# A two-layer decoder trunk on one core: last expert in four strips, w_pg split and router loads elsewhere, a turn of h ahead of a unit's low part

## The chip, the core and the metric

One core of a Trainium2 chip runs the whole program: TensorE (PE, with its weight loads PEld), VectorE (DVE), ScalarE (ACT), GpSimd (POOL) and SyncE (SP), whose queue issues the weight loads. The metric is device microseconds (us) of one execution, lower is better.

## The reference, cut to what matters

256 tokens of width 1024 go through two layers. Each layer is a token mixer, a mixture of experts and a gated per-layer embedding, each added to the residual `h`.

```python
for i in range(DEPTH):                      # 2
    h = h + mixer(rmsnorm(h, norm_mix[i]))  # even: conv + attention, odd: gMLP (w_in_odd, w_out_odd)
    h = h + hier_moe(rmsnorm(h, norm_ffn[i]), ...)   # 32 experts, top-2 of one group of 8
    gate = sigmoid(rmsnorm(h, norm_pl[i]) @ w_pg[i])
    h = h + gate * (p[i] @ w_pe[i])
return rmsnorm(h, final_norm)
# one expert: he = silu(x @ w1[e]) * (x @ w3[e]); y += comb[:, e] * (he @ w2[e])
```

## The kernel before

All code is emitted in one fixed order; each engine gets its instructions in the order in which the program writes them. Weights stream through 25 tiles of 1 MB ("units"), loaded on SP's queue in the order of use (`add_unit`, `emit_loads`); a unit is loaded as soon as the planned number of tiles allows it (`pos["hold"]`).

**Splitting.** The dense products are made of fp32r matmuls with x and w each as high and low part (high·high, low·high, high·low, `mm3`). Each unit of `w_pg` and of the odd mixer is therefore split ahead of use: the high part is a rounding copy on ACT (L130 or L132, `hi`), the low part a subtraction on DVE (L139 or L142, `lo`). `ahead(n)` splits units until `n` (by default `AHEAD = 2`) beyond the number already taken are split; `take` hands out the next unit and raises that number by one. A `w_pg` unit is split in four pieces of 512 columns.

**Mixture of experts (`moe`).** The 32 experts go in eight rounds `q` of four. Each round multiplies the gathered tokens with w1 and w3 (`up`, L923), forms the hidden values `he` (L954), turns them (`turn_hidden`, L960, L963) and multiplies with w2 (`down`, L976). The four experts of a round use four column strips of the array, 32 rows of output each. The result, weighted with the gates, is scattered into the accumulators `acc` by a matmul with the selection matrix (`scatter`, L994 and L996). The eight matmuls of a round's scatter are kept in a list `extra` and are emitted after the next round's `up` with w3. After the last round the kernel weights the output into `oF` (L1105, ACT), splits the first `w_pg` unit between the two halves, and adds with `sums` (L1117) and `add_h` (L448) to `h`.

**Per-layer part (`per_layer`, `proj_rows`).** `h` is turned on PE (L376), its high part `xTH` copied on ACT (L388), its low part `xTL` made on DVE (L392). The turn of the first 512 columns is done at the end of `moe`, that of the second 512 (`hook0`) inside the first `proj_rows`. `proj_rows` takes two units, i = 0 and i = 1; for each it does the token halves tt = 0 and tt = 1. `mid` (the function `rest`: the last `sums`, two `add_h`, two squares L347, rstd L369 and L370) stands between tt = 0 and tt = 1 of unit i = 0, and `hook0` inside tt = 1 of unit i = 0; unit i = 1 needs the columns that `hook0` turns. Unit 1 of `w_pg` is split ahead of i = 0, unit 2 ahead of i = 1.

**Odd mixer.** Its input is turned by `turn_next` (DVE scale L386, ACT copy L388, DVE low L392), the second half of it in `hook`, inside its first `proj_rows`. The first unit's low part (`piece[1]`, DVE L142) is emitted before. Its rstd runs on POOL (L370), behind the loads of `w_raw` and of the router's operands (`router_operands`, L330 to L334), which POOL issues. The activation `v` (L691) needs it.

Of the kernel before, what the change touches and what calls it, by code (L numbers as in the profile page):

```python
# [11 lines left out]
AF = mybir.ActivationFunctionType  # L12
# [34 lines left out]
def body(tc, x, p, norm_mix, norm_ffn, norm_pl, final_norm,  # L47
# [347 lines left out]
    def proj_cols(xH, xL, first=False):  # L395
# [16 lines left out]
                             skip_group_check=first)  # L412
        return ps.rearrange("p (c t) -> p c t", t=T)

    def proj_rows(xH, xL, tag="mm", hook=None, mid=None):

        pss = [psum("pr", tag)[:, 0:512] for _ in range(2)]
        for i in range(2):
            ahead()
            wh, wl = take(512, True)  # L420
            for tt in range(2):
                rows_part(pss[tt], xH, xL, wh, wl, i, tt, slice(0, 512),
                          hook if i == 0 and tt == 1 else None)
                if i == 0 and tt == 0 and mid is not None:
                    mid()
        return pss

    def rows_part(ps, xH, xL, wh, wl, i, tt, c, between=None):
# [245 lines left out]
        return nxt, lps, xc  # L674


    def odd_mixer(norm, xH, xL, w_sT, b_bc, make_w_sT, wr, hook):
        rb = None
        pos["hold"] = HOLD[6]
        v = [big("v0", [P, 4, 512]), big("v1", [P, 4, 512])]  # L680
        ssp = small("ssp", [P, 2, 4])
        for b in range(4):
            pss = proj_rows(xH, xL, ("mm", "y")[b % 2], hook=hook if b == 0 else None)
            if b == 0:
                r = norm.rstd()
            if b == 1:
                rb = norm.rows()
            if b == 2:
                make_w_sT()
            for tt in range(2):  # L690
                nc.scalar.activation(v[tt][:, b, :], pss[tt], AF.Gelu_apprx_tanh,  # L691
                                     scale=r[:, tt:tt + 1])
                sq = act("junk", [P, 512], BF16)
                nc.vector.scalar_tensor_tensor(sq, v[tt][:, b, :], 1.0 / 2048, v[tt][:, b, :],
                                               op0=ALU.mult, op1=ALU.mult,
                                               accum_out=ssp[:, tt, b:b + 1])
        ug = big("ug", [P, 2, 2, 2, T])
        yb = big("yb", [P, 2, 2, 2, T], F32R)

        def proj_u(n):  # L700
            ups = proj_cols(xH, xL)
            u, gt = ug[:, n % 2, 0], ug[:, n % 2, 1]
            nc.vector.tensor_tensor(u, ups, bt(rb), op=ALU.mult)
            nc.scalar.activation(u, u, AF.Gelu_apprx_tanh)
            return u, gt

        ss = small("ssv", [P, 2, 2])
        nc.vector.tensor_tensor(ss, ssp[:, :, 0:2], ssp[:, :, 2:4], op=ALU.add)
        rv = small("rv", [P, 2])
        rstd_of(rv, ss[:, :, 0], ss[:, :, 1])  # L710
        wms = big("wms", [P, 2, 8, P])
        for c in range(2):
            nc.vector.tensor_scalar(wms[:, c], w_sT, rv[:, c:c + 1], None, op0=ALU.mult)
        def gate(i, u):

            u, gt = u
            gps = psum("gps", "tp").rearrange("p (j t) -> p j t", t=T)
            for j in range(2):
                dt = 2 * i + j
                for c in range(2):  # L720
                    vs = slice((dt % 4) * P, (dt % 4) * P + P)
                    nc.tensor.matmul(gps[:, j, c * P:(c + 1) * P], v[c][:, dt // 4, vs],  # L722
                                     wms[:, c, i, :], start=True, stop=True)
            for j in range(2):
                dt = 2 * i + j
                bb = b_bc[:, i, :].unsqueeze(1).to_broadcast([P, 2, P])
                nc.vector.scalar_tensor_tensor(
                    gt[:, j, :].rearrange("p (c t) -> p c t", t=P),
                    gps[:, j, :].rearrange("p (c t) -> p c t", t=P),
                    cols[:, gv_c + dt:gv_c + 1 + dt], bb, op0=ALU.mult, op1=ALU.add)  # L730
            nc.vector.tensor_tensor(gt, gt, u, op=ALU.mult)
            yH, yL = yb[:, i % 2, 0], yb[:, i % 2, 1]
            nc.scalar.copy(yH, gt)
            nc.vector.tensor_tensor(yL, gt, f(yH), op=ALU.subtract)
            return [(yH[:, j, :], yL[:, j, :]) for j in range(2)]

        u = proj_u(0)
        ys = gate(0, u)
        u = proj_u(1)
        ops = [psum("ops", "y") for _ in range(2)]  # L740
        pos["hold"] = HOLD[3]
        nxt = Norm()
        for i in range(8):
            ys_next = gate(i + 1, u) if i < 7 else None
            if i == 6:
                pos["hold"] = HOLD[7]
                emit_loads()
            if i < 7:
                out_acc(ops, ys, i == 0, False, more=i == 6)
            else:  # L750
                lps, xc = finish_mixer(1, ops, ys, nxt, wr)
            if i < 6:
                u = proj_u(i + 2)
            if i == 5:
                pos["hold"] = HOLD[5]
                emit_loads()
            ys = ys_next
        return nxt, lps, xc
# [26 lines left out]
    def moe(li, norm, lps, xc, br):  # L785
# [142 lines left out]
        def places(q):  # L928

            c = slice((q % 2) * P, (q % 2 + 1) * P)  # L930
            s = S[q // 2]
            ps = psum("sl", "tp")
            for tt in range(2):
                nc.tensor.matmul(ps[:, 0:EPG + 1], s[:, tt, c], comb[:, tt, q // 2, :],
                                 start=(tt == 0), stop=(tt == 1))
            for tt in range(2):
                nc.tensor.transpose(ps[:, 128 + tt * P:128 + (tt + 1) * P], s[:, tt, c], ident)
            gt = small("gts", [P, 2])
            nc.vector.tensor_copy(gt[:, 1:2], ps[:, EPG:EPG + 1])
            nc.vector.scalar_tensor_tensor(small("gjunk", [P, EPG]), ps[:, 0:EPG], 1.0,  # L940
                                           own[:, q % 2, :], op0=ALU.mult, op1=ALU.mult,
                                           accum_out=gt[:, 0:1])
            st = act("ST", [P, T], F32R)
            nc.scalar.copy(st, ps[:, 128:128 + T])  # L944
            return gt, st

        def silu(ps, gt):
# [15 lines left out]
            nc.scalar.copy(gs, tp[:, 0:256].rearrange("p (j t) -> p j t", t=P))  # L963
            return gs

        def down(gs, after=None):
            pss = []
            first, ts = take_raw(4, D)
            for n in range(2):
# [3 lines left out]
                for j in range(2):  # L973
                    for e in range(4):
                        s = slice(e * CAP, (e + 1) * CAP)
                        nc.tensor.matmul(ps[s, :], gs[:, j, s], ts[e][:, j, c], start=(j == 0),  # L976
                                         stop=(j == 1))
                if after is not None:
                    after(ps, n)
            drop_raw(first, 4)  # L980
            return pss

# [77 lines left out]
        for q in range(NQ):  # L1060
# [9 lines left out]
            if q == PE_AT:  # L1070
                pe = big("pe", [P, 2, D])
                pT = turn_p(ptok)
                wpe = take(D, True)
                for n in range(2):
                    for tt in range(2):
                        extra.append(lambda n=n, tt=tt: embed(pT, wpe, pe, n, tt))
            p3 = up(3, q, take_raw(4, DE), 4)
            he = hidden(sl, p3)
            if q == 0:
# [13 lines left out]
                emit_loads()  # L1093
        pos["hold"] = HOLD[2]

        gs = turn_hidden(he)
        oF = big("oF", [P, D])
        gt, st = pl.pop(NQ - 1)
        st = f(st)
        nxt = Norm()  # L1100
        first = []

        def after(ps, n):
            c = slice(n * 512, (n + 1) * 512)
            nc.scalar.activation(oF[:, c], ps, AF.Copy, scale=gt[:, 0:1])  # L1105

            if n == 0:
                first.extend(split_pieces(pos["split"], apart=True))
                pos["split"] += 1
            for j in (2 * n, 2 * n + 1):  # L1110
                first[j][0]()
                if n == 0:
                    first[j][1]()

        def sums(tt, n):
            ps = acc[tt][:, n * 512:(n + 1) * 512]
            nc.tensor.matmul(ps, st[:, tt * P:(tt + 1) * P], oF[:, n * 512:(n + 1) * 512],  # L1117
                             start=False, stop=True, skip_group_check=True)
            return ps
        down(gs, after)  # L1120
        xH = big("xTH", [P, KD, T], F32R)
        xL = big("xTL", [P, KD, T], F32R)
        pss = [sums(0, 0), sums(1, 0)]
        add_h(pss[0], 0, 0)
        nxt.square(0, 0)
        add_h(pss[1], 1, 0)
        low0 = turn(0, 0, xH, xL)
        pss.append(sums(0, 1))
        low1 = turn(1, 0, xH, xL)
        nxt.square(1, 0)  # L1130
        low0()
        first[2][1]()
        first[3][1]()
        low1()

        def rest():

# [10 lines left out]
    def per_layer(norm, pe, xH, xL, rest, turn_next=None):  # L1148
# [24 lines left out]
        def quarters(pss, n, piece=None):  # L1173
# [9 lines left out]
                    nc.vector.tensor_tensor(hg[:, tt, c], h[:, tt, c], g[:, c], op=ALU.mult)  # L1183
                nxt.square(tt, n)
            if piece is not None:
                piece[1]()

        pss = proj_rows(xH, xL, "mm", hook=hook0, mid=rest)
        r = norm.r
# [77 lines left out]
    def turn_next(tt, n):  # L1267
        if not xT:
# [8 lines left out]
    nc.gpsimd.dma_start(w_raw, w_s_odd[0].rearrange("g t s -> t g s"))  # L1277
    nc.gpsimd.dma_start(b_bc.rearrange("p g t -> p (g t)"),
                        b_s_odd.rearrange("o g t -> o (g t)").to_broadcast([P, 1024]))
    wr, br = router_operands(1)  # L1280

    def make_w_sT():
        causal = act("causal", [P, P])
        nc.vector.tensor_tensor(causal, upper_b, ident, op=ALU.add)
# [7 lines left out]
    def hook():  # L1292
        for t in range(2):
            turn_next(t, 1)

    norm, lps, xc = odd_mixer(norm, xT["h"], xT["l"], w_sT, b_bc, make_w_sT, wr, hook)
    pe, norm, pxH, pxL, rest = moe(1, norm, lps, xc, br)
    per_layer(norm, pe, pxH, pxL, rest)
    ctx.close()

# [24 lines left out]
```

## Time and profile before

| | us |
|---|---|
| three runs | 743.07, 744.91, 745.07 (median 744.91) |
| the profiled execution, its own time | 743.51 |
| its span, first to last instruction | 741.5 |
| PE busy | 665.1 (90%) |
| DVE busy | 289.3 (39%) |
| ACT busy | 233.3 (31%) |
| mean granted TensorE clock | 0.963 |
| SP's weight queue | 255.35 MB, 85.4% of 16 engines' span |

The profiled execution's time is 2.0 us more than its span. Its records are on a clock that starts with the first instruction. Layer 0's experts end near 320, the odd mixer runs from about 340 to 500, layer 1's experts end near 705, and the rest is the last per-layer part and the final norm.

### The profile page before, as it was taken

How to read it: one execution, taken by the hardware profiler on the slowest of the kernel's cores; microseconds unless marked ns; L12 is line 12 of the kernel's file. 1: busy time of each engine (PE TensorE's matmuls, PEld its weight loads, DVE VectorE, ACT ScalarE, POOL GpSimd, SP SyncE). 2: the span in 40 equal slices, each digit the busy share in tenths (PEclk: the TensorE clock that was granted, in tenths of full speed). 3: DMA queues.
4: the chain of work that ended last, by engine and by line, in shares of the span. 5: the costliest groups of instructions: out<-in, count | busy, mean ns of one | idle time of the engine just before them, and what ended most of it. 6: DMA issues, size and time to landing. Idle time of an engine off the chain costs nothing.

```text
span 741.5 us, 12330 instructions
## 1 busy us (share of the span) xinstructions
PE 665.1 (90%) x5268; PEld 491.2 (66%) x5268; DVE 289.3 (39%) x482; ACT 233.3 (31%) x338; POOL 20.2 (3%) x37
## 2 busy tenths in 40 slices
PE   8999998988889778799999999999898987977795
PEld 8989988754465534358789999987574653633365
DVE  6748733221121210157667765634121220200076
ACT  6446524111112010067543443443101022010084
POOL 3100000000000000000100000000000000000000
PEclk9999999999999998899999999999999999989799
DMA  9994598999999999999971645499999999999931
GB/s 339 367 420 180 173 428 375 382 426 426 423 427 426 426 428 423 425 408 401 378 244 54 198 162 209 146 417 426 426 426 425 426 426 425 427 426 425 420 136 57
DMA packets 61163, 259.18 MB, mean 350 GB/s; under 512 B 4308, under 2 KB 22896, under 8 KB 36272
## 3 DMA queue, kind: packets, MB, share of 16 engines
q1 hardware_dynamic: 59888, 255.35, 85.4%
q0 software_dynamic: 1072, 2.47, 0.9%
q8 instruction: 43, 0.70, 0.3%
q10 hardware_dynamic: 144, 0.52, 0.2%
q14 instruction: 16, 0.13, 0.0%
HBM read 257.28 MB, written 1.05 MB: 348 GB/s over the span
## 4 chain that ended last, share of the span: by engine, by line
PE 58%; DMA 30%; DVE 5%; issue 3%; ACT 3%; POOL 1%; POOLq 0%; SPq 0%; ACTq 0%; DVEq 0%
DMA raw<-in_moe_w_dram 27%; PE pc L411 14%; PE ops L260 9%; PE hps L923 8%; PE gat L865 8%; PE pr L260 6%; PE yps L976 3%; DMA raw<-in_w_pe_dram 3%; DVE wl L139 1%; PE gps L722 1%; PE tp L376 1%; PE lps L467 1%; PE acc L994 1%; PE acc L1117 1%; PE acc L996 1%
## 5 line engine op out<-in xcount | busy, mean ns | idle before, releaser
L923 PE MATMUL hps<-raw,xg 128*32 128x256 f32 x2048 | 141.1, 410 | 36.2 <-DMA raw<-in_moe_w_dram 21.4
L923 PEld LDWEIGHTS hps<-raw,xg 128*32 128x32 f32 x2048 | 69.3, 118 | 107.5 <-DMA raw<-in_moe_w_dram 30.9
L142 DVE TENSOR_TENSOR wl<-raw,wh 128x2048 fp32r<-128x2048 f32 (+1 forms) x45 | 95.7, 2147 | 16.6 <-ACT wh L132 15.2
L976 PE MATMUL yps<-raw,gHL 128*32 128x512 f32 x512 | 69.3, 621 | 23.7 <-ACT gHL L963 17.7
L132 ACT CAST wh<-raw 128x2048 fp32r<-128x2048 f32 (+1 forms) x41 | 74.1, 1826 | 12.2 <-DMA raw<-in_w_in_even_dram 5.7
L944 ACT CAST ST<-sl 128x256 fp32r<-128x256 f32 x16 | 6.0, 372 | 223.6 <-DVE gjunk L940 221.7
L865 PE MATMUL gat<-S,h 128*128 128x256 f32 (+1 forms) x256 | 62.8, 404 | 0.0
L865 PEld LDWEIGHTS gat<-S,h 128*128 128x128 f32 x256 | 62.0, 336 | 1.1 <-issue 0.8
L976 PEld LDWEIGHTS yps<-raw,gHL 128*32 128x32 f32 x512 | 17.0, 113 | 64.3 <-issue 29.7
L987 DVE SCALAR_TENSOR_TENSOR o<-yps,gts,o 128x512 fp32r<-128x512 f32 x28 | 20.2, 748 | 88.7 <-ACT o L986 87.7
L868 DVE TENSOR_TENSOR xg<-gat,gffn 128x512 f32<-128x512 f32 x32 | 22.1, 692 | 61.2 <-PE gat L865 57.6
L260 PE MATMUL pr<-wh,xTH 128*128 128x512 f32 (+1 forms) x152 | 40.8, 390 | 1.6 <-ACT xTH L388 1.3
L411 PE MATMUL pc<-xTH,wh 128*128 128x256 f32 x288 | 42.1, 290 | 0.1
L411 PE MATMUL pc<-xTH,wl 128*128 128x256 f32 x288 | 40.5, 284 | 0.0
L411 PE MATMUL pc<-xTL,wh 128*128 128x256 f32 x288 | 40.3, 283 | 0.0
L260 PE MATMUL pr<-wl,xTH 128*128 128x512 f32 (+1 forms) x152 | 39.6, 383 | 0.4 <-DVE wl L142 0.4
L954 DVE TENSOR_TENSOR he<-sl,hps 128x256 f32<-128x256 f32 x16 | 6.7, 422 | 83.0 <-PE hps L923 83.0
L260 PE MATMUL pr<-wh,xTL 128*128 128x512 f32 (+1 forms) x152 | 39.1, 379 | 0.0
L411 PEld LDWEIGHTS pc<-xTH,wh 128*128 128x128 f32 x288 | 38.5, 196 | 0.9 <-ACT xTH L521 0.3
L986 ACT ACTIVATE o<-yps,gts 128x512 fp32r<-128x512 f32 x28 | 18.2, 684 | 63.6 <-PE yps L976 63.6
L411 PEld LDWEIGHTS pc<-xTH,wl 128*128 128x128 f32 x288 | 37.1, 192 | 0.3
L411 PEld LDWEIGHTS pc<-xTL,wh 128*128 128x128 f32 x288 | 37.1, 192 | 0.0
(228 smaller groups left out, 813.6 us busy)
## 6 DMA issues: line engine op xcount, KB each, us to landing
raw<-in_moe_w_dram SPq DMA_DIRECT2D x192, 1024.0 KB, 19.5
raw<-in_w_in_odd_dram SPq DMA_DIRECT2D x16, 1024.0 KB, 13.2
raw<-in_w_in_even_dram SPq DMA_DIRECT2D x11, 1024.0 KB, 11.7
raw<-in_w_pg_dram SPq DMA_DIRECT2D x8, 1024.0 KB, 12.4
raw<-in_w_out_odd_dram SPq DMA_DIRECT2D x8, 1024.0 KB, 6.1
raw<-in_w_out_even_dram SPq DMA_DIRECT2D x4, 1024.0 KB, 10.8
raw<-in_w_pe_dram SPq DMA_DIRECT2D x2, 1024.0 KB, 20.3
raw<-in_w_in_even_dram SPq DMA_DIRECT2D x2, 512.0 KB, 5.8
```

The costliest lines, as they stand in the source:

```text
L132: nc.scalar.copy(wh[:, c], raw[:, c])
L139: nc.vector.scalar_tensor_tensor(wl[:, c], raw[:, c], cols[:, col + j:col + j + 1], f(wh[:, c]), op0=ALU.mult, op1=ALU.subtract)
L142: nc.vector.tensor_tensor(wl[:, c], raw[:, c], f(wh[:, c]), op=ALU.subtract)
L260: nc.tensor.matmul(ps, x, w, start=start and i == 0, stop=stop and i == 3 * n - 1)
L376: nc.tensor.transpose(tp[:, j * P:(j + 1) * P], h[:, tt, k * P:(k + 1) * P], ident)
L411: nc.tensor.matmul(o, w, xx, start=st, stop=True if first else i % (3 * KD) == 3 * KD - 1, skip_group_check=first)
L865: nc.tensor.matmul(ps[:, k], src[:, tt, k0 + k, :], S[g][:, tt, c0:c1], start=(tt == 0 and k * m % 512 == 0), stop=True, skip_group_check= ...
L868: nc.vector.tensor_tensor(xg[g][:, k0:k0 + n, c0:c1], ps, gffn[:, li, k0:k0 + n].unsqueeze(2).to_broadcast([P, n, m]), op=ALU.mult)
L923: nc.tensor.matmul(ps[e * CAP:(e + 1) * CAP, :], x[:, k, c:c + CAP], ts[e][:, k, :], start=(k == 0), stop=(k == KD - 1))
L976: nc.tensor.matmul(ps[s, :], gs[:, j, s], ts[e][:, j, c], start=(j == 0), stop=(j == 1))
L986: nc.scalar.activation(o[:, 0, c], ps, AF.Copy, scale=gt[:, 0:1])
L987: nc.vector.scalar_tensor_tensor(o[:, 1, c], ps, gt[:, 0:1], f(o[:, 0, c]), op0=ALU.mult, op1=ALU.subtract)
```

## The change

1. In the last round (`q == NQ - 1`) the scatter of the round before is emitted ahead of `up` with w3.
2. The last `down` is written out: three experts in three strips over both halves, evacuated unweighted (ACT and DVE); then the fourth expert in four strips of 256 columns, one column quarter of the output for each strip, evacuated by ACT and DVE in 32-row copies. The gate goes into the selection matrix `st` (`places`).
3. The first `w_pg` unit is split after the first `sums`, not between the halves of `down`; the squares of the first columns come after the turns.
4. In the per-layer part's first `proj_rows`, `ahead(1)` stands ahead of i = 0 and a full `ahead()` directly after `mid`.
5. The low part of the odd mixer's second unit goes into `lows` and is emitted at the end of `hook`, after the turns; the second unit's products are reordered (all with the high part of w first).
6. The router's loads of layer 1 are emitted after the odd mixer's `norm.rstd()`.

```diff
     def proj_rows(xH, xL, tag="mm", hook=None, mid=None):
...
-            ahead()
+            ahead(1 if mid is not None and i == 0 else None)
             wh, wl = take(512, True)
+            if hook is not None and lows and i == 1:
+
+                for lo in (0, 1):
+                    for tt in range(2):
+                        s = slice(tt * P, (tt + 1) * P)
+                        for x, w in ((xH, wl),) if lo else ((xH, wh), (xL, wh)):
+                            for k in range(4):
+                                nc.tensor.matmul(pss[tt], x[:, 4 + k, s], w[:, k, :], start=False,
+                                                 stop=lo == 1 and k == 3)
+                lows.clear()
+                continue
             for tt in range(2):
                 rows_part(pss[tt], xH, xL, wh, wl, i, tt, slice(0, 512),
                           hook if i == 0 and tt == 1 else None)
                 if i == 0 and tt == 0 and mid is not None:
                     mid()
+                    ahead()
...
             if b == 0:
                 r = norm.rstd()
+                late["r"] = router_operands(1)
...
-            nc.scalar.copy(st, ps[:, 128:128 + T])
+            if q < NQ - 1:
+                nc.scalar.copy(st, ps[:, 128:128 + T])
+            else:
+
+                nc.scalar.activation(f(st), ps[:, 128:128 + T], AF.Copy, scale=gt[:, 0:1])
...
+            while q == NQ - 1 and extra:
+                pop()
             p3 = up(3, q, take_raw(4, DE), 4)
...
-        def after(ps, n):
+        fourth, ts = take_raw(4, D)
+        three = slice(0, 3 * CAP)
+        for n in range(2):
             c = slice(n * 512, (n + 1) * 512)
-            nc.scalar.activation(oF[:, c], ps, AF.Copy, scale=gt[:, 0:1])
-
-            if n == 0:
-                first.extend(split_pieces(pos["split"], apart=True))
-                pos["split"] += 1
-            for j in (2 * n, 2 * n + 1):
-                first[j][0]()
-                if n == 0:
-                    first[j][1]()
+            ps = psum("yps", "mm")
+            for j in range(2):
+                for e in range(3):
+                    s = slice(e * CAP, (e + 1) * CAP)
+                    nc.tensor.matmul(ps[s, :], gs[:, j, s], ts[e][:, j, c], start=(j == 0),
+                                     stop=(j == 1))
+            (nc.scalar.copy, nc.vector.tensor_copy)[n](oF[three, c], ps[three, :])
+        s = slice(3 * CAP, P)
+        qs = [psum("yq", "tp")[:, 0:256] for _ in range(2)]
+        for j in range(2):
+            for i in range(4):
+                nc.tensor.matmul(qs[i % 2][i * CAP:(i + 1) * CAP, :], gs[:, j, s],
+                                 ts[3][:, j, i * 256:(i + 1) * 256], start=(j == 0),
+                                 stop=(j == 1))
+        for i in range(4):
+            (nc.scalar.copy, nc.vector.tensor_copy)[i % 2](
+                oF[s, i * 256:(i + 1) * 256], qs[i % 2][i * CAP:(i + 1) * CAP, :])
+        drop_raw(fourth, 4)
...
-        down(gs, after)
+
+        first = split_pieces(pos["split"], apart=True)
+        pos["split"] += 1
...
         add_h(pss[0], 0, 0)
-        nxt.square(0, 0)
+        first[0][0]()
+        first[1][0]()
         add_h(pss[1], 1, 0)
+        first[0][1]()
+        first[1][1]()
         low0 = turn(0, 0, xH, xL)
         pss.append(sums(0, 1))
+        low0()
+        first[2][0]()
+        first[3][0]()
         low1 = turn(1, 0, xH, xL)
-        nxt.square(1, 0)
-        low0()
         first[2][1]()
         first[3][1]()
         low1()
+        for tt in range(2):
+            nxt.square(tt, 0)
...
             if piece is not None:
-                piece[1]()
+                lows.append(piece[1])
...
-    wr, br = router_operands(1)
...
     def hook():
         for t in range(2):
             turn_next(t, 1)
+        for low in lows:
+            low()
```

## Rows read from the trace of the kernel before

**Rows 1.** Windows by stage: us; PE, PEld, DVE, ACT, POOL busy; clock; DMA share; GB/s.

```profile
398.00:494.00 96.00, 96.00 (x637) 88.35 (x636) 61.47 (x64) 39.54 (x35) 0.69 (x1) 1.00 0.53 190
510.00:690.00 180.00, 151.97 (x1460) 91.52 (x1459) 32.75 (x88) 23.57 (x49) 1.30 (x2) 0.95 1.01 426
717.00:729.00 12.00, 12.00 (x58) 10.10 (x58) 10.55 (x16) 9.43 (x18) 0.45 (x1) 1.00 0.01 2
```

**Rows 2.** Timeline of layer 1's last round (start, us, engine, line, what).

```profile
688.18 0.75 DVE L987 SCALAR_TENSOR_TENSOR o<-yps,gts,o 128x512 fp32r<-128x512 f32 x1 [2.09 <-ACT o L986]
...
692.25 5.95 PE L923 MATMUL hps<-raw,xg 128*32 128x256 f32 x58 [1.66 <-DMA raw<-in_moe_w_dram]
...
698.12 0.50 PE L994 MATMUL acc<-o,ST 128*128 128x512 f32 x1
...
698.23 0.42 DVE L954 TENSOR_TENSOR he<-sl,hps 128x256 f32<-128x256 f32 x1 [9.30 <-PE hps L923]
...
699.85 0.40 PE L996 MATMUL acc<-o,ST 128*128 128x512 f32 x1
...
700.57 0.37 ACT L963 COPY gHL<-htp 128x256 f32<-128x256 f32 x1 [12.42 <-PE htp L960]
...
702.18 0.16 PEld L976 LDWEIGHTS yps<-raw,gHL 128*32 128x32 f32 x8 [1.04 <-DMA raw<-in_moe_w_dram]
702.64 0.13 PEld L976 LDWEIGHTS yps<-raw,gHL 128*32 128x32 f32 x4 [0.30 <-issue]
...
705.74 0.30 PEld L1117 LDWEIGHTS acc<-oF,ST 128*128 128x128 f32 x2 [0.84 <-ACT wh L130]
```

**Rows 3.** Timeline of layer 0's last round: three experts' strips, no fourth.

```profile
315.78 1.06 PE L976 MATMUL yps<-raw,gHL 128*32 128x512 f32 x6 [0.52 <-ACT gHL L963]
```

**Rows 4.** Timeline from layer 1's `sums` to the second unit of `proj_rows`.

```profile
707.76 0.69 DVE L448 TENSOR_TENSOR h<-h,acc 128x512 f32<-128x512 f32 x1 [0.17 <-PE acc L1117]
...
710.74 2.55 ACT L130 ACTIVATE wh<-raw,cols 128x512 fp32r<-128x512 f32 x4
...
711.49 2.74 DVE L139 SCALAR_TENSOR_TENSOR wl<-raw,cols,wh 128x512 fp32r<-128x512 f32 x4
...
714.14 1.28 DVE L448 TENSOR_TENSOR h<-h,acc 128x512 f32<-128x512 f32 x2
714.92 0.63 ACT L347 ACTIVATE junk<-h 128x512 bf16<-128x512 f32 x1 [1.62 <-DVE h L448]
...
716.30 1.05 ACT L388 CAST xTH<-tp 128x512 fp32r<-128x512 f32 x2
...
716.92 1.19 PE L260 MATMUL pr<-wh,xTH 128*128 128x512 f32 x4
```

**Rows 5.** Windows: the end of layer 0's routing, and the gather after it.

```profile
121.30:123.40 2.10, 0.33 (x5) 0.22 (x4) 1.65 (x8) 0.00 (x0) 0.00 (x0) 1.00 1.00 414
123.80:126.80 3.00, 3.00 (x16) 3.00 (x16) 0.00 (x0) 0.00 (x0) 0.00 (x0) 0.50 1.01 426
```

**Rows 6.** Timeline at the start of the odd mixer.

```profile
354.14 2.28 DVE L142 TENSOR_TENSOR wl<-raw,wh 128x2048 fp32r<-128x2048 f32 x1
...
357.73 1.19 PE L260 MATMUL pr<-wh,xTH 128*128 128x512 f32 x4 [1.26 <-ACT xTH L388]
...
363.37 0.89 POOL L331 DMA_DIRECT2D wr<-in_router_f_dram  x1 [5.42 <-issue]
363.71 0.15 DVE L369 SCALAR_TENSOR_TENSOR msq<-ss 128x2 f32<-128x2 f32 x1
...
365.37 0.72 POOL L370 TENSOR_TENSOR rstd<-msq,mhalf 128x2 f32<-128x2 f32 x1
...
366.12 1.27 ACT L691 ACTIVATE v<-pr,rstd 128x512 f32<-128x512 f32 x2 [3.35 <-POOL rstd L370]
...
369.23 1.20 PE L260 MATMUL pr<-wh,xTH 128*128 128x512 f32 x4 [0.32 <-ACT wh L132]
...
371.56 1.20 PE L260 MATMUL pr<-wl,xTH 128*128 128x512 f32 x4 [0.22 <-DVE wl L142]
```

More of the change, by code (lines that the diff above doesn't have):

```diff
@@ L413, in proj_cols @@
         return ps.rearrange("p (c t) -> p c t", t=T)
+    lows = []
     def proj_rows(xH, xL, tag="mm", hook=None, mid=None):
@@ L674, in even_mixer, with odd_mixer @@
         return nxt, lps, xc
-    def odd_mixer(norm, xH, xL, w_sT, b_bc, make_w_sT, wr, hook):
+    def odd_mixer(norm, xH, xL, w_sT, b_bc, make_w_sT, late, hook):
         rb = None
@@ L750, in odd_mixer @@
             else:
-                lps, xc = finish_mixer(1, ops, ys, nxt, wr)
+                lps, xc = finish_mixer(1, ops, ys, nxt, late["r"][0])
             if i < 6:
@@ L964, in turn_hidden, with down @@
             return gs
-        def down(gs, after=None):
+        def down(gs):
             pss = []
@@ L977, in down @@
                                          stop=(j == 1))
-                if after is not None:
-                    after(ps, n)
             drop_raw(first, 4)
@@ L1097, in moe @@
         oF = big("oF", [P, D])
-        gt, st = pl.pop(NQ - 1)
-        st = f(st)
+        st = f(pl.pop(NQ - 1)[1])
         nxt = Norm()
-        first = []
-        def after(ps, n):
+        fourth, ts = take_raw(4, D)
+        three = slice(0, 3 * CAP)
+        for n in range(2):
             c = slice(n * 512, (n + 1) * 512)
-            nc.scalar.activation(oF[:, c], ps, AF.Copy, scale=gt[:, 0:1])
-            if n == 0:
-                first.extend(split_pieces(pos["split"], apart=True))
-                pos["split"] += 1
-            for j in (2 * n, 2 * n + 1):
-                first[j][0]()
-                if n == 0:
-                    first[j][1]()
+            ps = psum("yps", "mm")
[16 more added lines that the diff above has]
+        drop_raw(fourth, 4)
         def sums(tt, n):
@@ L1294, in hook @@
             turn_next(t, 1)
-    norm, lps, xc = odd_mixer(norm, xT["h"], xT["l"], w_sT, b_bc, make_w_sT, wr, hook)
-    pe, norm, pxH, pxL, rest = moe(1, norm, lps, xc, br)
+        for low in lows:
+            low()
+    norm, lps, xc = odd_mixer(norm, xT["h"], xT["l"], w_sT, b_bc, make_w_sT, late, hook)
+    pe, norm, pxH, pxL, rest = moe(1, norm, lps, xc, late["r"][1])
     per_layer(norm, pe, pxH, pxL, rest)
```

## The prediction

> **What bounds the kernel now.** I read first the table of stages. In the odd mixer PE is busy for all of its 96 us at full clock, while the DMA engines have half their time free; in the experts it is the other way round, the weight stream runs at 426 GB/s with a DMA share of 1.01; in the last per-layer part PE is busy for 12.00 of 12.00 us again [rows 1]. So time moves only in two ways: what PE does or waits for after a layer's last w2 unit has landed, and what PE waits for in the odd mixer. A shift at layer 0's end is carried by the odd mixer to the start of layer 1's experts, whose length the stream sets; a shift after layer 1's last landing goes straight to the end. I then read the timeline of the three places that the change touches, engine by engine, each time asking what ended PE's wait.
>
> The sum is made against the profiled execution, 743.51 us (span 741.5 and 2.0 around it). It lies 1.4 under the median of the runs, 744.91, and within their spread of 2.0; I add nothing for that.
>
> **Parts 1 and 2: the last round.** In layer 1 PE waits until 692.25 for the fourth w3 unit. The second half of `o` is ready at 688.18 + 0.75 = 688.93, so the scatter that is moved ahead of `up` fits into that wait; it costs nothing there (if the unit were not late, it would cost its 2.0 us where it stands). At its old place it took from 698.12 to about 700.1, between `up` and the turn of `he` [rows 2]. Now the turn can start when `he` is done, 698.23 + 0.42 = 698.65, instead of at 699.85, so `down` starts at 699.85 instead of 701.0. Its units land 1 MB at 426 GB/s apart, 2.46 us; the fourth at 702.18, so the third at 699.7 and all three are there. Before, everything after 702.18 waited for the fourth: eight rounds of strips, a round every 0.13 + 0.30 = 0.43 us [rows 2], 3.44 us, until `sums` at 705.74.
>
> Now the three strips need the same eight rounds, 699.85 + 3.44 = 703.3. The fourth expert's four strips of 256 columns have no row of their own; half of 0.43 for half the columns, twice for each of two k halves, gives an estimate of 0.9: 704.2, long after its landing. Then comes a copy that nothing hides, since `sums` needs it: 0.37 on ACT (as gHL) or 0.42 on DVE (as he, both 128x256 [rows 2]), with some 0.15 to start. `sums` can begin at 704.8. Gain 0.95 us in each layer. Bounds: 0.4 if both strips' copies of an engine are awaited, 1.3 if start-up is nothing. Folding the gate into `st` replaces one ACT copy by another of that size, behind the same DVE result: nothing.
>
> The rounds of three strips are the uncertain row. The one stretch with three strips alone shows six matmul records (two rounds) in 1.06 us [rows 3], 0.86 by the rounds above plus a drain, so I take full overlap. The Trainium skill ("TensorE: Matmul & The Clock Gate", section "Measured speedup vs the span model") gives a speedup of only 2.38 for three column strips; by it the three strips would take 4.3 us instead of 3.44, and the sum below would be 0.9 us higher in each layer.
>
> **Parts 3 and 4: splitting w_pg.** Here I count from the start of `sums`, T (705.74 before). Before, unit i = 1 of `proj_rows` began at 716.92, T + 11.2, and PE was hardly idle on the way; unit 1's casts on ACT (710.74) and low parts on DVE (711.49) ran beside PE's first products [rows 4]. In the changed order:
>
> DVE ends the second `add_h` at T + 2.7 (707.76 + 0.69). Behind it now stand four low parts of the first unit and two xTL, which partly stood before `sums`: six at 0.69 (2.74 / 4) = 4.1, until T + 6.85. PE in that time loses about 0.2 for xTL and the last wh piece, so the last `sums` ends near T + 7.5. The two `add_h` of `rest` at 0.64 [rows 4] follow: the first until T + 7.5, the second from T + 7.7 (after `sums`) to 8.35. ACT's second square then runs from about T + 8.5 to 9.2 (two squares took 716.30 - 714.92 = 1.38).
>
> Now comes the point. `ahead()` after `mid` is called when one unit has been taken, and splits to two beyond: units 1 **and** 2. So eight casts of 2.55 / 4 = 0.64 us stand on ACT, 5.1 us, from T + 9.2 to 14.3. Behind them, in ACT's order, stand the two xTH copies of `hook0`, 1.05 for both [rows 4]. Before, only unit 1's casts were ahead of them, and those were done while DVE was still busy; unit 2's came after. The first xTH is done at T + 14.9. PE has finished both token halves and the eight transposes at T + 11.1, and its next product needs that copy. DVE has the eight low parts ahead of xTL as well, one 0.69 after its cast; xTL comes at about T + 16.0, 0.2 after PE wants it. So PE stands still for 3.8 us, and unit i = 1 begins 3.7 later than T + 11.2 and ends 3.9 later. In both layers. Unit 2 is then split early, but PE had no wait for it before (12.00 of 12.00 busy [rows 1]), so nothing comes back.
>
> Bounds for that stall: 3.4 if PE is late by 0.4 itself, 4.6 if ACT starts 0.7 later behind the squares. I take 3.9, nearest to the rows.
>
> A wait also has a price after it. After a stretch with 0.33 of 2.10 us busy, the granted clock was 0.50 for three us of full PE work, 1.2 instead of 2.4 GHz [rows 5]; three us at half speed lose 1.5. In the changed kernel PE does nothing for 3.8 us and then has dense work at once, so I add 1.5 in each layer (bounds 0 and 2.5).
>
> **Part 5: the turn in the odd mixer.** PE waited 1.26 us at 357.73 for xTH, whose DVE scale stood behind a low part of 2.28 [rows 6]. With the turn first, xTH is there at about 356.4, when PE comes. But the two turns take DVE until about 359.2 (each a scale, a wait for the copy, a low part: some 2.05), the unit's low part then until 361.5; PE, reordered, has done its sixteen products with the high part at 360.3 and waits 1.2 for it. The stall changes its place and its size hardly: I take 0 (bounds: 1.3 gained, 0.3 lost). The next unit's low part on DVE follows at the same time as before.
>
> **Part 6: the router's loads.** POOL issues them with long pauses (5.42 us before one) and takes rstd at 365.37 only, though its input is ready at 363.71 + 0.15; ACT stands 3.35 us before `v`, and the casts behind `v` arrive late at PE, which waits at 369.23 and 371.56 [rows 6]. Without the loads, rstd comes about 1.5 us earlier, and both waits go. They are 0.32 and 0.22 us on PE, with slower starts behind them; between 0.5 and 1.4 I take 0.9. The four loads then stand behind rstd on POOL; the next thing there is the rstd of `v`, which needs the whole first half of the odd mixer, and the operands are wanted only at its end, over 100 us later. That covers them; without the cover a pause of 5 to 6 us each would show.
>
> **Sum.** Each layer: -0.95 + 3.9 + 1.5 = +4.45. Twice that, -0.9 for part 6: +8.0. 743.5 + 8.0 = 751.5 us, slower.
>
> **Rivals.**
> (a) *The clock holds after the stalls.* For it: the wait of 1.04 us at 702.18 was followed by rounds at full speed [rows 2]. Against: what stands in [rows 5], and the length of 3.8. 743.5 + 2 x 2.95 - 0.9 = 748.5; with the clock falling after one of two, 750.0.
> (b) *Only one unit is split after `mid`,* if I miscount `ahead`. ACT would be free at T + 11.75, xTH at 12.4, a stall of 1.3 and about 1.5 lost per layer: 743.5 + 2 x 0.55 - 0.9 = 743.7, no change. The count in the code speaks against it.
> (c) *The copies are not held up, and the change does what its parts promise,* because the casts find idle time on ACT before the squares. Then -2 x 0.95 - 0.9 = -2.8: 740.7, faster. It decides when the stall is under 1.4 us per layer, that is when no more than about four of the eight casts stand ahead of the copies. Against it: ACT keeps its written order in the trace, it stood 3.35 us before `v` with casts right behind [rows 6].
> (d) *Three strips do not overlap fully:* 1.06 for two rounds [rows 3] makes 4.24 instead of 3.44, 0.8 more per layer, 753.1. The 1.06 contains a drain, so I give it little. The 2.38 of the Trainium skill (same page and section) points the same way; that the three experts alone took 1.06 rather than 0.86 does not settle it.
>
> **Chances.** The forecast 0.46 (own range 750 to 754); (a) 0.27; (d) and other losses beyond it 0.10; (b) and partial stalls 0.08; (c) 0.09. A change of 0.3%, 2.2 us, is about what this measurement can tell. Faster is (c), 0.09; within it (b), 0.08; slower the rest, 0.83. The range from 746.5 to 755.5 holds the first two, most of (d) and half-size stalls.
>
> **What would show it.** In layer 1: the scatter before 692, `sums` near 704.8, eight casts L130 in a row right after the squares with xTH behind them, PE idle for 3 to 4 us with ACT xTH as what ended it, the same near 331 to 335 in layer 0, and a granted clock of 0.5 after each. At 357 PE's wait shrinks and one of about 1.2 for a low part follows; `v` starts near 364.7. It is wrong if xTH of `hook0` follows the squares directly, or if PE has other work there.

## The result and the profile after

The changed kernel takes 752.12 us in the median of four runs (750.65 to 753.77), against 744.77 in four runs of the kernel before: a ratio of 1.0104 with a 95% interval of [1.0074, 1.0134], so about 1% slower. Its profiled execution took 753.17 us (span 751.4). The forecast was 751.5, in a range from 746.5 to 755.5. Every ratio below is to runs of the kernel before that were made together with those of the kernel in question.

Between the two profiled executions the span grows by 9.9 us. Marks that both traces have, in order, share it out (`rb` is the small product L361 in the odd mixer, the gather the first product of layer 1's experts with the selection matrix):

| stretch, in each kernel from mark to mark | before | after | difference |
|---|---|---|---|
| start to `sums` of layer 0 | 320.88 | 321.24 | +0.4 |
| `sums` to unit i = 1 of `proj_rows`, layer 0 | 11.19 | 14.64 | +3.45 |
| unit i = 1 to `rb` in the odd mixer | 43.25 | 44.17 | +0.9 |
| `rb` to the gather of layer 1 | 129.76 | 130.20 | +0.4 |
| that gather to `sums` of layer 1 | 200.66 | 199.90 | -0.8 |
| `sums` to unit i = 1, layer 1 | 11.18 | 14.65 | +3.5 |
| unit i = 1 to the first store of the output | 18.50 | 20.47 | +2.0 |
| first store to the end | 6.08 | 6.13 | +0.05 |

First the timeline of the changed kernel in layer 1's last round (start, duration, engine, line, what; in brackets the idle time before it and what ended it); it answers to [rows 2].

```profile
692.00 0.50 PE L1013 MATMUL acc<-o,ST 128*128 128x512 f32 x1 [0.21 <-DVE o L1004]
...
696.94 6.51 PE L938 MATMUL hps<-raw,xg 128*32 128x256 f32 x58 [1.80 <-DMA raw<-in_moe_w_dram]
...
703.49 0.42 DVE L973 TENSOR_TENSOR he<-sl,hps 128x256 f32<-128x256 f32 x1 [11.54 <-PE hps L938]
...
704.56 0.37 ACT L982 COPY gHL<-htp 128x256 f32<-128x256 f32 x1 [13.40 <-PE htp L979]
704.99 0.15 PEld L1128 LDWEIGHTS yps<-raw,gHL 128*32 128x32 f32 x6 [0.71 <-ACT gHL L982]
...
705.44 0.12 PEld L1128 LDWEIGHTS yps<-raw,gHL 128*32 128x32 f32 x3 [0.31 <-issue]
...
708.45 1.04 PE L1135 MATMUL yq<-raw,gHL 128*32 128x256 f32 x14
...
709.54 0.75 ACT L1139 COPY oF<-yq 32x256 f32<-32x256 f32 x2 [2.00 <-PE yq L1135]
709.59 0.88 DVE L1139 COPY oF<-yq 32x256 f32<-32x256 f32 x2 [0.22 <-PE yq L1135]
710.15 1.95 PE L1145 MATMUL acc<-oF,ST 128*128 128x512 f32 x4 [0.67 <-DVE oF L1139]
```

The scatter is over before the fourth w3 unit lands at 696.94, the turn and `down` follow `he` at once, a round of three strips takes 0.12 + 0.31 = 0.43 us like one of four, and the last copies (0.75 / 2 on ACT, 0.88 / 2 on DVE) stand bare before `sums`, which waits for one of each, as forecast. From the fourth unit's landing to `sums` it is 13.21 us, against 13.49 before. In layer 0 it is 321.24 - 308.74 = 12.50, against 320.88 - 307.51 = 13.37. The difference between the layers is `up`: 6.51 us here, at a granted clock of 0.55, and 3.64 in layer 0, at 1.00:

```profile
308.74 3.64 PE L938 MATMUL hps<-raw,xg 128*32 128x256 f32 x58 [1.82 <-DMA raw<-in_moe_w_dram]
```

Now the timeline of the changed kernel from layer 1's squares to the second unit, the answer to [rows 4].

```profile
718.65 0.63 ACT L347 ACTIVATE junk<-h 128x512 bf16<-128x512 f32 x1 [0.56 <-DVE h L462]
...
719.28 4.99 ACT L130 ACTIVATE wh<-raw,cols 128x512 fp32r<-128x512 f32 x8
...
719.53 1.03 PE L376 MATMUL tp<-ident,h 128*128 128x128 f32 x8
...
720.02 5.39 DVE L139 SCALAR_TENSOR_TENSOR wl<-raw,cols,wh 128x512 fp32r<-128x512 f32 x8 [0.45 <-ACT wh L130]
...
720.32 1.17 PE L260 MATMUL pr<-wl,xTH 128*128 128x512 f32 x4
724.18 1.05 ACT L388 CAST xTH<-tp 128x512 fp32r<-128x512 f32 x2
...
724.80 1.20 PE L260 MATMUL pr<-wh,xTH 128*128 128x512 f32 x4 [3.31 <-ACT xTH L388]
...
725.33 1.28 DVE L392 TENSOR_TENSOR xTL<-tp,xTH 128x512 fp32r<-128x512 f32 x2
726.07 0.87 PEld L260 LDWEIGHTS pr<-wh,xTL 128*128 128x128 f32 x4 [0.51 <-DVE xTL L392]
```

The second square ends, and eight casts follow in one row of 4.99 us. The xTH copy stands behind them in ACT's order, and PE, which has done the eight transposes and the last products of the first unit by 721.49 (720.32 + 1.17), waits 3.31 us for it. The low part xTL comes late as well: the products with it start 726.07 - 724.80 = 1.27 us after the first product of the unit, against 717.95 - 716.92 = 1.03 before. Layer 0 has the same rows: eight casts from 330.37, xTH at 335.26, and again a wait of 3.31. Windows of the changed kernel over this wait and the products after it, in both layers (us; PE, PEld, DVE, ACT, POOL busy; granted clock; DMA share; GB/s), show what follows.

```profile
331.60:335.80 4.20, 0.97 (x5) 0.45 (x3) 4.20 (x8) 4.20 (x9) 0.00 (x0) 1.00 1.05 404
336.00:339.40 3.40, 3.33 (x10) 2.38 (x11) 1.69 (x3) 1.80 (x3) 0.00 (x0) 0.73 1.05 404
339.40:342.80 3.40, 3.40 (x13) 2.69 (x13) 1.36 (x2) 0.69 (x1) 0.00 (x0) 0.77 1.05 410
720.50:724.70 4.20, 0.99 (x5) 0.47 (x3) 4.20 (x8) 4.20 (x9) 0.00 (x0) 1.00 0.00 0
725.00:728.40 3.40, 3.33 (x11) 2.33 (x11) 2.62 (x5) 3.37 (x6) 0.00 (x0) 0.75 0.02 5
728.40:731.80 3.40, 3.40 (x13) 2.72 (x12) 3.29 (x6) 1.48 (x3) 0.00 (x0) 0.75 0.00 0
```

With the wait over, PE is busy throughout, but part of that time runs at the lower level (1.2 GHz): 3.40 x 0.27 + 3.40 x 0.23 = 1.7 us lost in layer 0, 2 x 3.40 x 0.25 = 1.7 in layer 1.

Last, the timeline of the changed kernel in the odd mixer, the answer to [rows 6].

```profile
362.31 1.20 PE L430 MATMUL pr<-wh,xTH 128*128 128x512 f32 x4
...
367.22 2.11 PE L430 MATMUL pr<-wl,xTH 128*128 128x512 f32 x8 [0.81 <-DVE wl L142]
...
369.59 0.71 POOL L370 TENSOR_TENSOR rstd<-msq,mhalf 128x2 f32<-128x2 f32 x1 [14.54 <-DVE msq L369]
...
380.05 0.38 PE L361 MATMUL rb<-ident,rstd 128*128 128x128 f32 x2
```

The wait of 1.26 us for xTH is gone, one of 0.81 for the low part stands behind it, rstd follows its input at once, and no product waits until `rb`. From the first product of the odd mixer to `rb` it is 380.05 - 355.19 = 24.86 us, against 375.32 - 349.42 = 25.90 before: 1.04 us less.

### The profile page after: what moved, and what is told of

Its sections match the earlier page's. It is cut to its first block, busy times and chain, and to the rows that moved or that the text cites. A ratio compares the mean times of both kernels' runs of the same rounds, so it can differ in the third digit from the quotient of the medians.

```text
span 751.4 us, 12377 instructions
## 1 busy us (share of the span) xinstructions
PE 667.8 (89%) x5284; PEld 493.5 (66%) x5284; DVE 292.4 (39%) x488; ACT 234.1 (31%) x340; POOL 20.2 (3%) x37
## 3 DMA queue, kind: packets, MB, share of 16 engines
HBM read 257.28 MB, written 1.05 MB: 344 GB/s over the span
## 4 chain that ended last, share of the span: by engine, by line
PE 59%; DMA 31%; DVE 5%; ACT 3%; issue 1%; POOLq 0%; POOL 0%; SPq 0%; ACTq 0%; DVEq 0%
DMA raw<-in_moe_w_dram 30%; PE pc L411 13%; PE pr L260 10%; PE ops L260 9%; PE hps L938 8%; PE gat L880 7%; PE yps L995 2%; DVE wl L139 2%; PE acc L1145 1%; PE lps L481 1%; PE gps L737 1%; PE yps L1128 1%; PE tp L376 1%; DVE wl L142 1%; PE acc L1011 1%
## 5 line engine op out<-in xcount | busy, mean ns | idle before, releaser
L995 PE MATMUL yps<-raw,gHL 128*32 128x512 f32 x448 | 56.0, 596 | 22.0 <-ACT gHL L982 17.2
L995 PEld LDWEIGHTS yps<-raw,gHL 128*32 128x32 f32 x448 | 13.7, 109 | 54.3 <-issue 25.2
```

## The experiments

The theory that they test: the eight casts ahead of the copies are the loss, through PE's wait and through the clock after it; the last round gives back some 0.9 us in each layer, part 6 about 1 us once, part 5 nothing. The rivals are that one unit's casts cost as much, that the wait costs nothing beyond itself, and that the loss lies in another part.

**One unit instead of two behind `mid`.**

```diff
                     mid()
-                    ahead()
+                    ahead(1)
```

> The changed kernel, but only w_pg unit 1 is split after mid; unit 2 is split ahead of i = 1, as before. Theory (the eight casts ahead of hook0's xTH copies are the cost): four casts of 0.63 fewer, so the first xTH comes 2.5 us earlier; PE's wait ahead of i = 1 falls from 3.3 to about 0.9 us, the granted clock stays at 1.0 after it, and each layer is 4 us shorter: 744.5 (743.5 to 746). Rival (the fourth expert's strips and the copies in front of sums are the cost): about 752, as the changed kernel.

743.14 us, a ratio of 1.0001 [0.9986, 1.0016] to the kernel before; the median lies 0.4 us below the range expected. Between the medians one argument is worth 752.12 - 743.14 = 9.0 us, but they are of two sets of runs, and the ratios make it 7.7. In the traces it is 58.81 - 54.52 = 4.29 us from `sums` to `rb` in layer 0 and 35.12 - 30.89 = 4.23 from `sums` to the first store in layer 1, together 8.5. The timeline of this kernel in layer 1:

```profile
713.16 2.55 ACT L130 ACTIVATE wh<-raw,cols 128x512 fp32r<-128x512 f32 x4
...
715.62 1.04 ACT L388 CAST xTH<-tp 128x512 fp32r<-128x512 f32 x2
...
716.23 1.20 PE L260 MATMUL pr<-wh,xTH 128*128 128x512 f32 x4 [0.88 <-ACT xTH L388]
```

Four casts leave a wait of 0.88 us, after which the clock stays at 1.00. From the fourth w3 unit to `sums` it is 12.46 and 12.53 us, so the last round gives its 0.91 and 0.96 here. That gain, the remaining wait and part 6 come to about nothing in sum.

**The split at its old place in `proj_rows`** (part 4 undone).

```diff
-            ahead(1 if mid is not None and i == 0 else None)
+            ahead()
...
                     mid()
-                    ahead()
```

> The changed kernel with the old place of the splits in the per-layer part: unit 1 ahead of i = 0, unit 2 ahead of i = 1. Theory: no casts stand between the squares and hook0's xTH copies. But unit 1's low parts then stand on DVE ahead of the two add_h of rest, which come about 2.7 us later, so PE's transposes wait: i = 1 at about T + 12.5 instead of T + 14.65, no fall of the clock. 744.5 (743 to 746.5). Rival (the cost is in the other parts): about 752.

745.81 us, 1.0016 [0.9997, 1.0035], inside what was expected. Without part 4 most of the loss is gone, so it does not come from the first unit's new place (part 3). But the old order does not bring the other gains to the end either: two rows of this kernel's timeline in layer 1 show unit 1's low parts on DVE, with `add_h` behind them, and PE's transposes wait 0.88 us for that.

```profile
713.05 2.74 DVE L139 SCALAR_TENSOR_TENSOR wl<-raw,cols,wh 128x512 fp32r<-128x512 f32 x4 [0.43 <-ACT wh L130]
...
716.53 1.16 PE L376 MATMUL tp<-ident,h 128*128 128x128 f32 x8 [0.88 <-DVE h L461]
```

In its layer 0 a part of the last `down` ran at a lower clock (0.78 from 316.0 to 321.5, against 1.00 in the changed kernel), and `sums` came 14.20 us after the fourth w3 unit; in layer 1 it was 12.55.

**Part 4 alone on the kernel before.**

```diff
-            ahead()
+            ahead(1 if mid is not None and i == 0 else None)
...
                     mid()
+                    ahead()
```

> The kernel before with part 4 alone: ahead(1) ahead of i = 0 and a full ahead() after mid. Theory: eight casts between the squares and hook0's xTH copies; PE waits about 3.4 us ahead of i = 1 in each layer and runs 1.7 us longer after it at a granted clock of 0.5. 5 us per layer: 755 (752 to 757), so more than the whole change costs. Rival (the cost comes from other parts, the casts are hidden): 744 to 746.

754.54 us, 1.0153 [1.0136, 1.0170]: this edit alone costs more than the whole change. The timeline of this kernel in layer 1 shows the row of eight and the wait, the same in layer 0 (at 335.20):

```profile
719.10 5.00 ACT L130 ACTIVATE wh<-raw,cols 128x512 fp32r<-128x512 f32 x8
...
724.62 2.07 PE L260 MATMUL pr<-wh,xTH 128*128 128x512 f32 x4 [3.31 <-ACT xTH L388]
```

Behind the same wait less is lost here than in the changed kernel: from unit i = 1 to `rb` it is 44.56 us against 43.25 before, from unit i = 1 to the first store 19.84 against 18.50, so 1.3 us in each layer for the clock and a late xTL together.

**The wait filled with work that nobody needs.** The changed kernel, with products into an unused tile just where PE waits.

```diff
             wh, wl = take(512, True)
+            if mid is not None and i == 1:
+                fill = psum("fill", "y")
+                for _ in range(56):
+                    nc.tensor.matmul(fill[:, 0:P], ones_b, ones_b, start=True, stop=True)
```

> The changed kernel with 56 added matmuls of ones (128 columns, bf16, into an unused accumulator) just ahead of unit i = 1, where PE waits. They add no result; they keep PE busy for about 3.1 of the 3.3 us. Theory (1.7 us of each layer's loss is the half clock after the wait): the clock stays at 1.0 and i = 1 to the end is 1.7 us shorter in each layer: 748.8 (747.5 to 750). Rival (the whole loss is the wait itself and late xTL): 752, or a little more if the added matmuls run past the wait.

750.18 us, 1.0085 [1.0051, 1.0118], 0.2 us above the range expected. Unit i = 1 begins as late as in the changed kernel (14.69 us after `sums`), so the copies are as late as they were; only the clock differs. The same windows of this kernel, to be set beside those above:

```profile
331.60:335.80 4.20, 4.01 (x61) 3.53 (x59) 4.20 (x8) 4.20 (x8) 0.00 (x0) 1.00 1.05 405
336.00:339.40 3.40, 3.33 (x14) 2.43 (x14) 1.58 (x3) 1.85 (x4) 0.00 (x0) 1.00 1.06 407
...
725.00:728.40 3.40, 3.40 (x16) 2.79 (x16) 3.29 (x5) 2.49 (x5) 0.00 (x0) 1.00 0.02 5
```

From `sums` to `rb` it is 57.22 us instead of 58.81, from `sums` to the first store 33.56 instead of 35.12: 1.6 us in each layer is the price of the clock. In the medians the difference is 1.9 us instead of 3.2, and the intervals overlap; the trace settles it, the times alone would not.

**The other parts, each alone on the kernel before:** part 6, part 5, and part 1 (`while q == NQ - 1 and extra: pop()` ahead of `up`).

> The kernel before with part 6 alone, the router's loads behind the odd mixer's rstd. Theory: rstd runs 0.3 us after its input, v begins 1.5 us earlier, PE's waits for ACT wh and DVE wl in the second block go, and all after it is 1.0 us earlier: 743 (ratio about 0.9986). Rival (POOL's lateness is hidden): no such shift in the trace, ratio 1.000.

Part 6: 742.47 us, 0.9991 [0.9981, 1.0000]. In the trace `sums` to `rb` falls from 54.44 to 53.31, by 1.13 us, since rstd now starts at once:

```profile
363.76 0.71 POOL L370 TENSOR_TENSOR rstd<-msq,mhalf 128x2 f32<-128x2 f32 x1 [13.66 <-DVE msq L369]
```

> The kernel before with part 5 alone, the turn ahead of the unit's low part and the products reordered. Theory: PE's wait of 1.26 us for xTH goes and a wait of about 0.8 to 1.2 us for the unit's low part comes, the second block begins at the same time within 0.2 us: ratio 1.000. Rival (the turn was the bound): 1.2 us less, ratio 0.9984.

Part 5: 742.29 us, 0.9985 [0.9976, 0.9995]. That is a miss, as the theory gave this part nothing. PE's waits change places as foreseen, in its timeline in the odd mixer:

```profile
361.42 2.12 PE L430 MATMUL pr<-wl,xTH 128*128 128x512 f32 x8 [0.81 <-DVE wl L142]
```

But `sums` to `rb` falls by 1.05, to 53.39. The timeline of POOL in the same kernel shows where it may come from:

```profile
346.86 0.95 POOL L1290 DMA_DIRECT2D w_raw<-in_w_s_odd_dram  x1 [14.27 <-PE pr L260]
348.73 0.56 POOL L1291 DMA_DIRECT2D wsb<-in_b_s_odd_dram  x1 [0.92 <-PE pr L260]
354.72 0.89 POOL L330 DMA_DIRECT2D wr<-in_router_c_dram  x1 [5.43 <-issue]
361.03 0.89 POOL L331 DMA_DIRECT2D wr<-in_router_f_dram  x1 [5.42 <-issue]
...
363.78 0.71 POOL L370 TENSOR_TENSOR rstd<-msq,mhalf 128x2 f32<-128x2 f32 x1 [0.77 <-DVE msq L369]
```

The load of `w_raw` goes out at 346.86; before, it stood at 348.83. The loads behind it move too, the router's by 2.34 us, so POOL has issued the last one at 363.0 and is free when rstd's input comes; rstd starts at 363.78, against 365.37. In the trace part 5 thus removes the same lateness of rstd as part 6, by another way.

> The kernel before with part 1 alone, the scatter ahead of the last up. Theory: he comes 1.8 us or more earlier, but down still waits for the fourth w2 unit and has 3.5 us of work behind its landing, so sums stays where it was, within 0.3 us of 13.4 after the fourth w3 unit's landing: ratio 1.000. Rival (the scatter's 2 us stood on the chain): sums 1.5 us earlier per layer, ratio 0.996.

Part 1: 744.62 us, 1.0018 [1.0007, 1.0028]. The scatter is early, but from the fourth w3 unit to `sums` it is still 13.37 and 13.51 us: in the timeline `down` starts sooner, and then waits 1.41 us for its last unit, behind which all rounds still stand.

```profile
699.48 1.20 PE L976 MATMUL yps<-raw,gHL 128*32 128x512 f32 x6 [0.52 <-ACT gHL L963]
702.09 3.62 PE L976 MATMUL yps<-raw,gHL 128*32 128x512 f32 x26 [1.41 <-DMA raw<-in_moe_w_dram]
```

Its runs are 1 us above those before; the one traced execution (span 741.4) does not show where.

**Why part 5 alone gains.** The idea: the load goes out earlier because of the place of its tile. The edit on the kernel before allocates `w_raw` ahead of `wsb`.

```diff
+    w_raw = big("w_raw", [P, 8, P])
     wsb = big("wsb", [P, 2, 8, P])
     w_sT, b_bc = wsb[:, 0], wsb[:, 1]
-    w_raw = big("w_raw", [P, 8, P])
```

> The kernel before with nothing changed but the order in which the two tiles wsb and w_raw are taken. Theory (part 5 alone gained because POOL's first load, of w_raw, could be issued 2 us earlier into a tile that came free earlier, so that the router's loads were through before rstd): w_raw's load goes out near 346.9 instead of 348.8, rstd runs 0.3 us after its input, and the second block and all after it come 1.0 us earlier, though PE's wait of 1.26 us for xTH stays: ratio 0.9986. Rival (part 5 gained on PE): no shift, ratio 1.000.

744.38 us, 1.0004 [0.9995, 1.0013]. The load goes out at 349.13, after the same wait of 16.23 us, and rstd is late as before (365.70). The swap did not set the load free, so it says nothing on what an earlier load brings. What in part 5 frees that tile sooner stays open.

**Parts 5 and 6 together on the kernel before.**

> The kernel before with parts 5 and 6. Theory: both remove the same lateness of rstd, so together they bring what each brings alone, the odd mixer's second product 1.05 us earlier: ratio 0.9986. Rival (each has a gain of its own): 2.1 us, ratio 0.997.

742.99 us, 0.9988 [0.9979, 0.9997]. `sums` to `rb` is 53.38, as with either alone (53.39 and 53.31): the two gains are one.

**A version with the copies ahead of the squares and of unit 2.** The changed kernel, where the casts of unit 1 follow the turns, three of its low parts follow `add_h`, the fourth the turns of `hook0`, the last squares and rstd follow the turns of `hook0`, and unit 2 stands ahead of i = 1.

```diff
                 if i == 0 and tt == 0 and mid is not None:
+                    pcs = split_pieces(pos["split"], apart=True)
+                    pos["split"] += 1
+                    for hi, _ in pcs:
+                        hi()
                     mid()
-                    ahead()
+                    for _, lo in pcs[:3]:
+                        lo()
+                    tail.append(pcs[3][1])
...
                 turn(t, 1, xH, xL)()
+            for lo in tail:
+                lo()
+            tail.clear()
+            for t in range(2):
+                norm.square(t, 1)
+            norm.rstd()
```

> The changed kernel with the per-layer part's first unit pair in another order: unit 1's four casts directly after the turns of moe, the squares of the first columns behind them, three of unit 1's four low parts behind the add_h of rest, then hook0's turns, the last low part, the squares of the second columns and rstd, and unit 2 ahead of i = 1 as before. Theory: no cast and no square stands between add_h and hook0's xTH copies, so i = 1 begins at about T + 11.2, 3.5 us earlier than in the changed kernel and 1 us earlier than with one unit after mid, in each layer; with the last round's and the router's gain 2 to 3 us under the kernel before: 741.5 (740.5 to 743). Rival (PE waits for other things there, low parts above all): as e1, 743 to 744.

742.67 us, 0.9984 [0.9972, 0.9996]. Unit i = 1 begins 11.2 us after `sums` without a wait, as before the change, and the last round keeps its gain. A new wait in the odd mixer takes part of it: 0.51 us for a cast at 350.41, since the load of the sigmoid's table now comes later on ACT. So the next kernel issues that table load ahead of the copies of `hook0`:

> The reordered kernel (e8) with the sigmoid's table load moved ahead of hook0's copies, where ACT stood idle for 1.26 us. Theory: the first sigmoid comes 1.3 us earlier, the casts behind it too, and the wait of 0.51 us on PE at the last w_pg unit's end of layer 0 goes: 0.6 us under e8, ratio to the kernel before about 0.9977. Rival (that wait has another cause): as e8, 0.9984.

741.03 us, 0.9964 [0.9951, 0.9978], the fastest of all, though its interval overlaps that of the reordered version. The wait of 0.51 us is gone, and `sums` to `rb` falls from 54.05 to 53.29. Its timeline in layer 1 shows the load where ACT has time, and the copy right behind it:

```profile
711.82 1.28 ACT L1183 ACT_TABLE_LOAD   x1
...
713.23 1.06 ACT L388 CAST xTH<-tp 128x512 fp32r<-128x512 f32 x2
```

Last, the reordered version without its early scatter (the `while` of part 1 taken out):

> The reordered kernel (e8) with the scatter of the round before back behind up, part 1 undone. Theory: he waits behind the scatter again, down starts 1.9 us later, and with the strips' own work and copies behind it sums comes 13.4 us after the fourth w3 unit, as in the kernel before, instead of 12.5; 0.8 us per layer: ratio about 1.0005. Rival (the strips alone bring the gain): 12.5 us and ratio 0.9984.

744.22 us, 1.0005 [0.9996, 1.0014], against 0.9984 with it. From the fourth w3 unit to `sums` it is 13.29 us in layer 0 and, with `up` at 6.40 us, 705.42 - 691.06 = 14.36 in layer 1. The strips without the early scatter gain nothing, as the early scatter without the strips gained nothing. Part 3 was not run alone.

## Why the prediction was right

**The eight casts (3.9 in each layer): right, and the main cost.** The count of `ahead` decided it. Four casts leave a wait of 0.88 us and no change of the time, eight a wait of 3.31 and some 8 to 9 us; part 4 alone is slower than the whole change. Measured were 3.45 and 3.47, with about 0.25 more where xTL comes late behind eight low parts: 3.7. PE stood still for 3.31 and not 3.8, since it came to the copy at 721.49 - 710.15 = 11.3 us after `sums` and not at 11.1, and the copy itself a quarter of a microsecond sooner. Filled PE time does not help the copies, an earlier copy does.

**The clock after the wait (1.5 in each layer): right.** The row of [rows 5] was enough to foresee it. In the changed kernel two readings give the price: 1.7 from the windows of the granted clock, 1.6 from the kernel whose wait was filled. With part 4 alone it was at most 1.3 behind the same wait; why it differs is open. It is the difference between forecast and rival (a), which falls with it. The wait of 1.04 us that spoke for (a) stands in the row of weight loads; PE itself was busy for 4.67 of the 4.90 us from 700.9.

**The last round (-0.95 in each layer): the mechanism right, the size conditional.** It gave 0.87 in layer 0 and 0.28 in layer 1 of the profiled execution; 0.91 and 0.96 in the kernel with one unit. The working took `up` as it stood. With `up` at 3.64 to 5.2 us the stream decides, and `sums` comes 12.4 to 12.6 us after the fourth unit, save in the layer 0 where `down` ran at the lower clock (14.20); at 6.51 us PE decides, and most of the gain is lost. That the two halves of this step need each other was in the working (the turn starts earlier, the three strips use it) and is shown by the kernels with one of them. The rounds of three strips took 0.43 us, so rival (d) falls. The Trainium skill ("TensorE: Matmul & The Clock Gate", section "Measured speedup vs the span model") gives a speedup of 2.38 for three column strips; an estimate by it is 0.43 x 3 / 2.38 = 0.54 us for a round, and the measured 0.43 decides here.

**Part 5 (0): right in the sum by luck, wrong on its own.** The wait for xTH went, and 0.81 came in place of the 1.2 expected. What the working didn't see is that with this edit POOL's load of `w_raw` goes out 2 us sooner. Alone, the part is worth 1.05 us in the trace. That parts 5 and 6 together bring no more than either shows that it is the gain that part 6 has already; the sum does not change, but no step of the working said so.

**Part 6 (-0.9): right.** 1.04 in the change and 1.13 alone in the trace. Its size is that of the noise in the times, so only the trace shows it.

**The sum.** The terms as measured, -0.87 - 0.28 + 2 x 3.7 + 2 x 1.7 - 1.05, make +8.6 (with 1.05 for parts 5 and 6), against +8.0 forecast; the gain of the last round was 0.75 less than forecast, the clock cost 0.4 more, the casts 0.4 less. The profiled executions differ by 9.7, the medians by 7.35. What the trace shows beside the terms lies in code that the change doesn't touch: +1.13 up to the first gather, +0.4 behind `rb`, and some -0.5 in layer 1's stream; no experiment tells it from the spread between executions. Rival (b) is the first experiment, whose 743.14 lies 0.6 below the 743.7 that it was given. Rival (c) falls with the wait of 3.31 us; it needed the casts to find idle time, and its 740.7 is about what the version with the early table load reaches (741.03) by taking the casts out of the way.

## What to carry to other kernels

When a split or a cast is moved behind other work, count all of its instructions on its engine up to the next copy that PE waits for, and with a "keep two ahead" helper count what it does at its new place, not at the old one. A wait of PE can cost more than its length: here 3.31 us of it were followed by 1.3 to 1.7 us lost to the lower granted clock, 0.88 us by none, and work put into the wait kept the clock up. Two edits that remove the same lateness don't add; measure them together before summing them, and look at the one mark behind both.

## What was not expected of the hardware

The clock of `up` in the last round differed between layers and executions of like code: 58 recorded products took 3.64 us in some, at a granted clock of 1.00, and 4.96 to 6.51 in others, at 0.55 to 0.73. The early scatter fills a part of PE's waits ahead of the fourth unit; the fast ones were seen in seven of the twelve last rounds that had the early scatter and the strips together, and in none of the sixteen others. Why seven and not twelve is open. Up to 5.3 us it hardly moved `sums`, since the stream came last.

Some loads issued by POOL came after pauses for which the profile shows no cause: 6.72 us ahead of the router's first load and 5.42 ahead of its second in the kernel before, but 2.18 ahead of the second in the changed kernel, and none ahead of its third and fourth. A small rstd behind them waits for its turn. A kernel whose first load went out 2 us sooner and one whose loads stand behind rstd gained the same.

The first gather came at 123.45 us before and 124.58 after, ahead of anything that the change touches, and at 123.3 to 125.1 in the other kernels. A difference of 1 us between two profiled executions can thus be none of the change's, and the terms above were read as stretches between marks for that reason.
